# Forget gates placed between the second pair's keys and queries, with work tiles from another buffer pool

## The chip, the cores and the metric

The kernel runs on one core of a Trainium2 chip. The metric is device time in microseconds (us) per execution. A core has five instruction queues that work side by side and wait for each other through semaphores: TensorE (PE; its weight loads are shown apart as PEld), VectorE (DVE), ScalarE (ACT), GpSimd (POOL) and SyncE (SP), which here only issues DMAs. Each engine takes its own queue strictly in order.

## The reference

One layer of a streaming encoder for 512 new positions and, beside them, 64 positions that continue a stream with 1024 cached ones. Two kinds of attention share one input projection; FoX is the one that the change touches. Its logits carry a forget gate per head, a running sum F of log-sigmoids:

```python
h = rmsnorm(x, g_attn)
z = h @ w_in
q, k, v, f_lin, q_c, c_kv, k_r = jnp.split(z, IN_SPLIT_POINTS, axis=-1)
logf = jax.nn.log_sigmoid(f_lin.astype(jnp.float32) + b_f.astype(jnp.float32))
f_past = jnp.cumsum(plogf32, axis=1)
f_new = jnp.sum(plogf32, axis=1, keepdims=True) + jnp.cumsum(logf, axis=1)
...
s = jnp.einsum('bqhd,bkhd->bhqk', q, k, preferred_element_type=jnp.float32) * (FOX_DIM ** -0.5)
s = s + jnp.transpose(fq, (0, 2, 1))[:, :, :, None] - jnp.transpose(fk, (0, 2, 1))[:, :, None, :]
p = jax.nn.softmax(jnp.where(mask, s, NEG), axis=-1)
```

The second kind (MLA) follows with its own latents, then the output projection, a gated convolution block with an up and a down projection, and a final norm. `logf`, keys, values and latents are outputs too.

## The kernel before

All matrices lie transposed, features on partitions and the 576 positions along a row. Every product is made exact to about float32 by splitting both factors into a leading half and a remainder. For weights this is `hilo`: a weight tile of 128x1024 is loaded into `wr` (L185), ScalarE copies the leading half into `wh` (L194), and VectorE or GpSimd, in turn, writes the remainder (L135). `in_tile` then makes one 128-row tile of the projection: 48 matmuls (L210), 24 for each half of the positions, into two PSUM banks. There are two `wr` and two `wh` buffers, and two banks of the kind `g`.

`fox_gemm(p)` projects a pair of heads: keys, queries, values, each `in_tile` followed by two evictions on VectorE (L450, L454, L457) into a `raw` tile. There are seven `raw` buffers. Eight `mix` buffers hold the input `x` first (`x_in`), later the rotary key, the gate logits `z`, the latent tiles (`latent`, L541, five of them) and the attention outputs.

`gates` makes F out of `z` on 8 partitions: ScalarE adds the bias (L560), VectorE takes the minimum of z and -z (L562), ScalarE its exponential (L564), VectorE 1 + e and its rounding error (L566, L567), GpSimd a subtraction (L568), ScalarE the logarithm (L569), VectorE the sum (L570) and `logf` (L572), then the scans (L577 for the new positions, L586 for the 64 of the running stream), and ScalarE and VectorE split the sums into halves: L580 and L581 into `Fh`, `Fl` (tiles `qr`), L589 and L590 into `Fs` (tile `cf`). SyncE copies rows of `Fh` and `Fl` into each head's score tile `A` (L510, L511, `fox_stack`); the sample scores read `cf` directly (L523 of `fox_sample_scores`), after the product of cached keys and query (L522). Head scores are L515, L516 and a mask (L359), in four blocks of query rows per head, 256, 256, 384 and 512 wide; ScalarE takes the exponentials (L326), and TensorE transposes the result (L375).

What sets the order: generators (`s_gemm`, `s_scores`, `s_values`, `s_sample_scores`, `s_sample_values`) write the parts of the program by due times, and that writing order is a priority. When the kernel is built, a scheduler orders each engine's queue by priority and by what it reckons to be ready, and gives each tile a buffer of its kind that is free. So moving a call moves its instructions on every queue, and others around them. `s_gemm` is the generator that calls `fox_gemm(1)` first and then `gates`.

Of the kernel before, what the change touches and what calls it, by code (L numbers as in the profile page):

```python
# [17 lines left out]
T = NP + NS  # L18
# [53 lines left out]
def build(nc, tc, io):  # L72
# [7 lines left out]
    def f(ap):  # L80
        return ap.bitcast(F32)
# [6 lines left out]
    def raw():  # L88

        if ffn[0]:  # L90
            rawn[0] += 1
            tag, bufs = FRAW[rawn[0] % len(FRAW)]
            return sb([P, 580], F32, tag, bufs)
        return sb([P, 580], F32, "raw", RAW)

    def mixt():
        return sb([P, T], F32, "mix", 8)
# [194 lines left out]
    def in_tile(u, M=P):  # L292
        hl = wload(io["w_in"][u], 1024)
        ps = psg()
        gemm(ps, M, hl, xhl, HA)
        return ps
# [147 lines left out]

    mixes = [None] * 8

    def fox_gemm(p):
        ps = k0 if p == 0 else in_tile(p)
        k = raw()
        evac(lambda d, p, c: V.tensor_tensor(d, p, R[:, c], op=ALU.mult), k, ps)  # L450
        G.dma_start(io["o_k"][p], k[:, :T])
        ps = in_tile(4 + p)
        q = raw()
        evac(lambda d, p, c: V.scalar_tensor_tensor(d, p, FOX_SCALE, R[:, c], op0=ALU.mult, op1=ALU.mult), q, ps)  # L454
        ps = in_tile(8 + p)
        v = raw()
        evac(lambda d, p, c: V.tensor_tensor(d, p, R[:, c], op=ALU.mult), v, ps)  # L457
        G.dma_start(io["o_v"][p], v[:, :T])
        return q, k, v
# [96 lines left out]
    fx = {0: fox_gemm(0)}  # L556
    gate = {}

    def gates():
        S.activation(z, z, AF.Identity, bias=bf)  # L560
        mn = raw()[:8, :T]
        V.scalar_tensor_tensor(mn, z, -1.0, z, op0=ALU.mult, op1=ALU.min)  # L562
        e = raw()[:8, :T]
        S.activation(e, mn, AF.Exp)  # L564
        up = raw()[:8, :T]
        V.tensor_scalar(up, e, 1.0, None, op0=ALU.add)  # L566
        V.tensor_scalar(mn, up, 1.0, None, op0=ALU.subtract)  # L567
        G.tensor_tensor(e, e, mn, op=ALU.subtract)  # L568
        S.activation(up, up, AF.Ln)  # L569
        V.tensor_tensor(up, up, e, op=ALU.add)  # L570
        logf = raw()[:8, :T]
        V.scalar_tensor_tensor(logf, z, 0.0, up, op0=ALU.min, op1=ALU.subtract)  # L572
        G.dma_start(io["o_logf"], logf)
        zero8 = sb([8, 2816], F32, "B", 2)
        G.memset(zero8, 0.0)
        fp = raw()[:8, :T]
        V.tensor_tensor_scan(fp[:, :NP], logf[:, :NP], zero8[:, :NP], 0.0, op0=ALU.add, op1=ALU.add)  # L577
        Fhl = sb([8, 2, T], F32R, "qr", 1)
        Fh, Fl = Fhl[:, 0], Fhl[:, 1]
        S.activation(Fh[:, :NP], fp[:, :NP], AF.Copy)  # L580
        V.tensor_tensor(Fl[:, :NP], fp[:, :NP], f(Fh[:, :NP]), op=ALU.subtract)  # L581
        lc = sb([8, 1152], F32, "sp", 1)
        G.dma_start(lc[:, :PAST], io["logf_c"])
        fs = sb([8, 1152], F32, "spt", 1)
        V.tensor_tensor_scan(fs[:, :PAST], lc[:, :PAST], zero8[:, :PAST], 0.0, op0=ALU.add, op1=ALU.add)
        V.tensor_tensor_scan(fs[:, PAST:KEYS], logf[:, NP:T], zero8[:, :NS], fs[:, PAST - 1:PAST], op0=ALU.add, op1=ALU.add)  # L586
        Fs = sb([72, 1152], F32R, "cf", 1)
        G.memset(f(Fs), 0.0)
        S.activation(Fs[0:8, :KEYS], fs[:, :KEYS], AF.Copy)  # L589
        V.tensor_tensor(Fs[64:72, :KEYS], fs[:, :KEYS], f(Fs[0:8, :KEYS]), op=ALU.subtract)  # L590
        gate.update(h=Fh, l=Fl, s=Fs)
# [151 lines left out]
    def s_gemm():  # L743
        for p in range(1, 4):
            if p >= 2:
                yield ("after", ("stack", 2 * (p - 2) + 1), 0)
            fx[p] = fox_gemm(p)
            if p == 1:
                gates()
            yield ("done", 23.1, ("up", p))  # L750
            if p == 1:
                for a in range(5):
                    latent(a)
                    if a == 2:
                        rope_key()
                    if a == 1:
                        acc_c = sq_sum(craw)
                    if a == 4:
                        acc_q = sq_sum(qcr)
                    yield ("done", 7.7, ("lat", a))  # L760
            if p == 2:
                latent_norm(craw, 256, C_GKV, acc_c)
                latent_norm(qcr, 384, C_GQ, acc_q)
                for a in range(2):
                    G.dma_start(io["o_lat"][a], craw[a])
        mla_keys()
        yield ("done", 0, ("keys", 0))
        for p in range(4):
            if p == 0:
                yield ("after", ("stack", 5), 0)  # L770
            else:
                yield ("after", ("stack", 6 + 2 * p - 1), 0)
            if p % 2 == 0:
                q_rope(p // 2)
                yield ("done", 2.2, ("rope", p))
            mla_up(p)
            yield ("done", 5, ("up", 4 + p))
# [320 lines left out]
```

## Time and profile before

| | us |
|---|---|
| median of 3 runs (807.28 to 808.03) | 807.97 |
| the profiled execution | 810.69 |
| its span, first to last instruction | 808.9 |
| TensorE busy in it | 772.8 |
| VectorE busy | 508.5 |
| ScalarE busy | 340.6 |
| GpSimd busy | 264.0 |

The profiled execution is one run of its own, with a time of its own; the rows below are from it. A busy TensorE is not a TensorE at its peak: the granted clock says at which of its two levels it ran. The share of busy time over the whole span mixes stages with different limits, so the rows are given by stage and by engine.

### The profile page before, as it was taken

To read this page: it belongs to the slowest core of one execution; us is meant where nothing else is said; L and a number is where in the kernel's file an instruction comes from. 1 tells how busy PE (TensorE), PEld (TensorE's weight loads), DVE (VectorE), ACT (ScalarE), POOL (GpSimd) and SP (SyncE) were. 2 spreads that over 40 slices of the span, in tenths; PEclk is the share of its full clock that TensorE was granted. 3 is DMA by queue.
4 is the path that set the end of the run, shared out by engine and by line. 5 is a ranking of instruction groups with operands and counts; after the bars stand their busy time and mean duration, and the time that the engine had idled before them with its cause. 6 is when DMAs were issued, how large, how long until landed. Compare 5 with 4: busy or idle time off the path is not lost.

```text
span 808.9 us, 14256 instructions
## 1 busy us (share of the span) xinstructions
PE 772.8 (96%) x5582; PEld 743.3 (92%) x5582; DVE 508.5 (63%) x941; ACT 340.6 (42%) x611; POOL 264.0 (33%) x390
## 2 busy tenths in 40 slices
PE   8898999999899989999999999999999999999994
PEld 8796899897789879999999999999999999999993
DVE  6838554878677763457867524676425667675356
ACT  7224652457667864124443212343113433433231
POOL 5134342336143230223333221433222343332034
PEclk9998999999999999999999999999999999999997
DMA  9373423545563741222222223222232222222313
GB/s 329 111 212 109 109 84 106 145 107 169 129 152 80 185 131 30 80 79 79 72 85 68 79 92 105 79 79 60 79 98 80 103 80 79 79 66 83 105 40 117
DMA packets 33811, 83.98 MB, mean 104 GB/s; under 512 B 6006, under 2 KB 9350, under 8 KB 33744
## 3 DMA queue, kind: packets, MB, share of 16 engines
q1 hardware_dynamic: 31520, 78.55, 32.6%
q0 software_dynamic: 1008, 3.19, 1.1%
q10 hardware_dynamic: 1216, 1.33, 0.5%
q8 instruction: 44, 0.72, 0.4%
q14 instruction: 23, 0.19, 0.1%
HBM read 64.12 MB, written 5.49 MB: 86 GB/s over the span
## 4 chain that ended last, share of the span: by engine, by line
PE 76%; DVE 10%; ACT 5%; DMA 3%; issue 3%; SPq 1%; POOL 1%; DVEq 0%; ACTq 0%; POOLq 0%
PE g L210 31%; PE s L210 19%; PE t L210 12%; PE g L438 3%; PE g L969 1%; DMA mix<-xT 1%; DVE B L382 1%; DVE xs L267 1%; PE s L720 1%; PE t L375 1%; ACT p L326 1%; PE s L969 1%; DMA A<-qr 1%; PE s L522 1%; DVE raw L135 1%
## 5 line engine op out<-in xcount | busy, mean ns | idle before, releaser
L210 PE MATMUL g<-xs,wh 128*128 128x288 f32 (+2 forms) x2028 | 281.1, 295 | 0.3 <-ACT spt L128 0.2
L210 PEld LDWEIGHTS g<-xs,wh 128*128 128x128 f32 x2028 | 271.1, 189 | 1.7 <-ACT spt L128 0.4
L194 ACT ACTIVATE wh<-wr 128x1024 fp32r<-128x1024 f32 (+4 forms) x106 | 99.8, 942 | 204.3 <-PE g L210 88.4
L135 POOL TENSOR_TENSOR wh<-wr,wh 128x1024 fp32r<-128x1024 f32 (+3 forms) x51 | 111.8, 2192 | 216.5 <-ACT wh L194 173.7
L210 PE MATMUL s<-xs,wh 128*128 128x320 f32 (+3 forms) x840 | 121.1, 300 | 2.3 <-DVE xs L267 2.3
L210 PEld LDWEIGHTS s<-xs,wh 128*128 128x128 f32 (+1 forms) x840 | 116.3, 188 | 2.7 <-ACT wh L194 1.8
L210 PE MATMUL t<-xs,wh 128*128 128x256 f32 (+3 forms) x576 | 83.9, 296 | 1.2 <-DVE xs L267 1.2
L210 PEld LDWEIGHTS t<-xs,wh 128*128 128x128 f32 (+1 forms) x576 | 79.1, 188 | 1.6 <-DVE xs L267 1.4
L135 DVE TENSOR_TENSOR wh<-wr,wh 128x1024 fp32r<-128x1024 f32 (+5 forms) x55 | 59.0, 1077 | 13.7 <-ACT wh L194 13.4
L892 POOL COPY KR<-raw 128x2 f32<-128x2 f32 x33 | 14.6, 443 | 94.1 <-DVE raw L890 94.1
L332 POOL TENSOR_SCALAR p<-p,small 128x128 f32<-128x128 f32 (+2 forms) x48 | 27.5, 575 | 50.9 <-DVE small L327 40.8
L896 DVE SCALAR_TENSOR_TENSOR raw<-raw,par 128x578 f32<-128x578 f32 x22 | 33.6, 1526 | 14.0 <-ACT raw L895 14.0
L326 ACT ACTIVATE p<-s,small 128x128 f32<-128x128 f32 (+1 forms) x64 | 33.6, 527 | 12.5 <-DVE small L361 9.2
L920 ACT ACTIVATE raw<-raw 128x578 f32<-128x578 f32 x22 | 15.1, 688 | 54.5 <-DVE raw L897 54.5
L382 DVE TENSOR_TENSOR B<-t,B 128x512 fp32r<-128x512 f32 (+1 forms) x64 | 29.9, 482 | 9.3 <-ACT B L128 9.2
L128 ACT ACTIVATE B<-t 128x512 fp32r<-128x512 f32 (+1 forms) x64 | 26.2, 435 | 17.1 <-PE t L375 16.4
L361 DVE TENSOR_REDUCE small<-s 128x1 f32<-128x128 f32 (+1 forms) x64 | 30.5, 480 | 4.3 <-PE s L359 2.9
L896 DVE SCALAR_TENSOR_TENSOR raw<-pq,par,raw 128x578 f32<-128x578 f32 x11 | 22.7, 2059 | 12.4 <-ACT raw L895 12.4
L375 PE MATMUL t<-ident,p 128*128 128x128 f32 x160 | 29.1, 277 | 1.0 <-DVE B L382 0.5
L890 DVE TENSOR_TENSOR raw<-s,R 128x256 f32<-128x256 f32 x22 | 9.3, 424 | 31.8 <-PE s L210 31.8
L438 PE MATMUL g<-spt,sv 128*128 128x128 f32 x216 | 26.7, 276 | 0.3 <-ACT spt L128 0.2
L438 PEld LDWEIGHTS g<-spt,sv 128*128 128x128 f32 x216 | 25.2, 192 | 1.1 <-ACT spt L128 0.6
(337 smaller groups left out, 1344.1 us busy)
## 6 DMA issues: line engine op xcount, KB each, us to landing
wr<-w_up SPq DMA_DIRECT2D x44, 512.0 KB
wr<-w_dn SPq DMA_DIRECT2D x24, 384.0 KB
wr<-w_in SPq DMA_DIRECT2D x16, 512.0 KB
A<-pq SPq DMA_DIRECT2D x32, 256.0 KB
mix<-xT SPq DMA_DIRECT2D x16, 288.0 KB
wr<-w_out SPq DMA_DIRECT2D x8, 512.0 KB
A<-pq SPq DMA_DIRECT2D x24, 128.0 KB
sk<-k_c SPq DMA_DIRECT2D x4, 512.0 KB
```

Source lines behind the costliest of these rows:

```text
L128: S.activation(dst, src, AF.Copy)
L135: (V if pick(kind) == "v" else G).tensor_tensor(dst, a, b, op=op)
L194: S.activation(hl[:, 0, a:b], r[:, a:b], AF.Copy)
L210: PE.matmul(ps[hf][:M, :w], lhsT=hl[:, wi, kc * M:(kc + 1) * M], rhs=acts[kc][:, xi, o:o + w], start=(kc == 0 and pi == 0), stop=(kc == n ...
L326: S.activation(p, src, AF.Exp, bias=nm, accum_out=sm[:, 0:1])
L332: (G if e == "g" else V).tensor_scalar(p, p, sm[:, 1:2], 1.0, op0=ALU.mult, op1=ALU.mult)
L361: V.reduce_max(nm[:, 0:1], s[:, :W], axis=AX.X, negate=True)
L375: PE.transpose(t[:, P * (i - j):P * (i - j + 1)], st["p"][i][:, P * j:P * (j + 1)], ident)
L382: V.tensor_tensor(ptj[:, 1, off:], t[:, :w], f(ptj[:, 0, off:]), op=ALU.subtract)
L438: PE.matmul(out, lhsT=v[:, j, :], rhs=spt[:, j, :], start=(j == 0), stop=(j == 8))
L896: V.scalar_tensor_tensor(t, u[:, 1:579], par[:, C_CW + 44 + ch:C_CW + 44 + ch + 1], t, op0=ALU.mult, op1=ALU.add)
L969: PE.matmul(ps[:, :w], lhsT=whl[m][:, wi, kc * P:(kc + 1) * P], rhs=g2[kc][:, xi, c], start=(kc == 0 and pi == 0), stop=(kc == n - 1 and p ...
```

## The change

`fox_gemm` takes a second argument, a function that it calls between the keys and the queries. For pair 1 (the second) `s_gemm` passes `gates`, which it called after the whole of `fox_gemm(1)` before. And the five work tiles of `gates` come from `mixt()`, the `mix` buffers, and no longer from `raw()`.

```diff
-    def fox_gemm(p):
+    def fox_gemm(p, between=None):
         ps = k0 if p == 0 else in_tile(p)
         k = raw()
         evac(lambda d, p, c: V.tensor_tensor(d, p, R[:, c], op=ALU.mult), k, ps)
         G.dma_start(io["o_k"][p], k[:, :T])
+        if between:
+            between()
         ps = in_tile(4 + p)
...
-        mn = raw()[:8, :T]
+        mn = mixt()[:8]
...
-        e = raw()[:8, :T]
+        e = mixt()[:8]
...
-        up = raw()[:8, :T]
+        up = mixt()[:8]
...
-        logf = raw()[:8, :T]
+        logf = mixt()[:8]
...
-        fp = raw()[:8, :T]
+        fp = mixt()[:8]
...
-            fx[p] = fox_gemm(p)
-            if p == 1:
-                gates()
+            fx[p] = fox_gemm(p, gates if p == 1 else None)
```

The two lines added in `fox_gemm` push the later lines down by two: from L450 on, a line of the kernel before has a number higher by 2 in the kernel after (L523 becomes L525), up to the call in `s_gemm`. The rest of the text uses the numbers of before. What this does to the queues is shown at three places.

TensorE, from the first product of cached keys and query to the first head scores. L210 are projection matmuls, L341 and L494 transposes of values, L523 the sample scores that read the gates' sums. Before:

```order
L522 MATMUL s<-sk,qb 128x320
L210 MATMUL g<-xs,wh 128x288 x144
L341 MATMUL t<-ident,raw 128x128 x4
L494 MATMUL t<-ident,raw 64x128
L210 MATMUL g<-xs,wh 128x288 x27
L341 MATMUL t<-ident,raw 128x128 x4
L210 MATMUL g<-xs,wh 128x288 x10
L494 MATMUL t<-ident,raw 64x128
L210 MATMUL g<-xs,wh 128x288 x11
L523 MATMUL s<-cf,sl 128x384 x2
L523 MATMUL s<-cf,sl 128x320
```

And after:

```order
L524 MATMUL s<-sk,qb 128x320
L210 MATMUL g<-xs,wh 128x288 x72
L341 MATMUL t<-ident,raw 128x128 x2
L210 MATMUL g<-xs,wh 128x288 x24
L341 MATMUL t<-ident,raw 128x128 x2
L496 MATMUL t<-ident,raw 64x128
L525 MATMUL s<-cf,sl 128x384 x2
L525 MATMUL s<-cf,sl 128x320
L527 LDWEIGHTS bfc
L527 MATMUL s<-bfc 128x64
L210 MATMUL g<-xs,wh 128x288 x48
L517 MATMUL s<-A 128x256
```

The sample scores stand behind 96 projection matmuls instead of 192, and 48 of the others stand between them and the first head's scores; the last 48 of the 192 stand between that head's blocks, 30 of them ahead of the second head.

VectorE, where the gates' first instructions stand (L450, L454 and L457 are evictions of keys, queries and values, L465 and L467 splits for a pair's scores). Before, behind the weight remainder for the second pair's values:

```order
L467 TENSOR_TENSOR pq<-raw,pq 128x512
L454 SCALAR_TENSOR_TENSOR raw<-g,R 128x288 x2
L465 TENSOR_TENSOR pq<-raw,pq 128x512
L457 TENSOR_TENSOR raw<-g,R 128x288
L562 SCALAR_TENSOR_TENSOR raw<-mix 8x576
L566 TENSOR_SCALAR raw<-raw 8x576
L567 TENSOR_SCALAR raw<-raw 8x576
L457 TENSOR_TENSOR raw<-g,R 128x288
```

And after, behind the weight remainder for its keys:

```order
L564 SCALAR_TENSOR_TENSOR mix<-mix 8x576
L469 TENSOR_TENSOR pq<-raw,pq 128x512
L459 TENSOR_TENSOR raw<-g,R 128x288
L467 TENSOR_TENSOR pq<-raw,pq 128x512
L568 TENSOR_SCALAR mix<-mix 8x576
L459 TENSOR_TENSOR raw<-g,R 128x288
L569 TENSOR_SCALAR mix<-mix 8x576
L450 TENSOR_TENSOR raw<-g,R 128x288
L572 TENSOR_TENSOR mix<-mix 8x576
L574 SCALAR_TENSOR_TENSOR mix<-mix 8x576
L579 SCALAR_TENSOR_TENSOR mix<-mix,B 8x512
L588 SCALAR_TENSOR_TENSOR spt<-mix,spt,B 8x64
```

The gates' first three instructions stood behind the queries' evictions and the split of the second pair (L467, L465) and now stand among the first pair's; L570 to L586 stand between the two evictions of the second pair's keys (the first L450 is in the fence, the second follows it).

ScalarE, from the first pair's last split (L464) on; L194 are leading halves of weights. Before, up to the first exponential of a head:

```order
L464 ACTIVATE pq<-raw 128x512
L564 ACTIVATE raw<-raw 8x576
L194 ACTIVATE wh<-wr 128x1024
L569 ACTIVATE raw<-raw 8x576
L580 ACTIVATE qr<-raw 8x512
L589 ACTIVATE cf<-spt 8x1088
L194 ACTIVATE wh<-wr 128x1024
L220 ACTIVATE raw<-mix 128x576
L326 ACTIVATE p_683,small<-s,small 128x128
```

And after, the gates' part:

```order
L466 ACTIVATE pq<-raw 128x512
L566 ACTIVATE mix<-mix 8x576
L194 ACTIVATE wh<-wr 128x1024
L571 ACTIVATE mix<-mix 8x576
L194 ACTIVATE wh<-wr 128x1024
L582 ACTIVATE qr<-mix 8x512
L591 ACTIVATE cf<-spt 8x1088
L468 ACTIVATE pq<-raw 128x512
L194 ACTIVATE wh<-wr 128x1024
```

Four gate instructions moved from between the weight halves of the first three latent tiles to between those of the second pair's queries and values. The third latent tile's half, which followed the gates' last cast, now follows the first head's exponentials and those of the first sample.

## Rows read from the trace of the kernel before

**Rows 1.** Stages: us; busy us of each engine (instructions), clock, DMA share, GB/s.

```profile
42.10:113.80 71.70, 67.04 (x471) 61.58 (x470) 45.05 (x108) 35.50 (x79) 30.83 (x39) 0.95 0.45 123
113.80:145.60 31.80, 31.80 (x242) 31.80 (x241) 12.80 (x16) 6.80 (x11) 7.70 (x8) 1.00 0.38 115
318.60:808.90 490.30, 476.81 (x3565) 474.36 (x3563) 291.29 (x460) 162.84 (x208) 152.33 (x239) 0.99 0.26 82
```

**Rows 2.** Timeline, TensorE: start us, us, instructions [idle before <-releaser].

```profile
41.72 19.48 PE L210 MATMUL g<-xs,wh 128*128 128x288 f32 x144
...
66.94 1.71 PE L210 MATMUL g<-xs,wh 128*128 128x288 f32 x11
71.79 0.90 PE L523 MATMUL s<-cf,sl 72*128 72x384 f32 x3 [3.13 <-DVE cf L590]
...
72.89 0.58 PE L515 MATMUL s<-A 128*128 128x256 f32 x1
...
79.24 0.60 PE L375 MATMUL t<-ident,p 128*128 128x128 f32 x4
80.38 0.50 PE L515 MATMUL s<-A 128*128 128x512 f32 x1 [0.53 <-ACT p L326]
...
82.68 0.35 PE L516 MATMUL s<-A 66*128 66x256 f32 x1 [0.49 <-DMA A<-qr]
```

**Rows 3.** Timeline, TensorE's weight loads, at the first head's scores.

```profile
72.89 0.29 PEld L515 LDWEIGHTS s<-A 128*128 128x128 f32 x1 [0.26 <-DVE sp L410]
```

**Rows 4.** One microsecond: TensorE busy us, granted clock, DMA share, GB/s.

```profile
78.00:79.00 1.00, 1.00 (x6) 0.50 1.01 213
```

**Rows 5.** Timeline, TensorE at the upper clock level, the same forms.

```profile
87.23 0.49 PE L375 MATMUL t<-ident,p 128*128 128x128 f32 x3
...
88.31 0.36 PE L515 MATMUL s<-A 128*128 128x256 f32 x1
...
88.67 0.42 PE L515 MATMUL s<-A 128*128 128x384 f32 x1
...
89.16 0.90 PE L210 MATMUL g<-xs,wh 128*128 128x288 f32 x5
...
90.38 0.39 PE L515 MATMUL s<-A 128*128 128x512 f32 x1
...
90.88 1.83 PE L210 MATMUL g<-xs,wh 128*128 128x288 f32 x12
```

**Rows 6.** Timeline, the gates' instructions and what stands around them.

```profile
35.20 0.76 ACT L560 ACTIVATE mix<-mix,bf 8x576 f32<-8x576 f32 x1
...
40.38 1.06 ACT L194 ACTIVATE wh<-wr 128x1024 fp32r<-128x1024 f32 x1 [2.83 <-issue]
...
41.70 2.42 POOL L135 TENSOR_TENSOR wh<-wr,wh 128x1024 fp32r<-128x1024 f32 x1
...
45.32 0.46 DVE L450 TENSOR_TENSOR raw<-g,R 128x288 f32<-128x288 f32 x1 [4.53 <-PE g L210]
...
48.52 1.06 ACT L194 ACTIVATE wh<-wr 128x1024 fp32r<-128x1024 f32 x1 [7.08 <-PE g L210]
...
49.61 1.23 DVE L135 TENSOR_TENSOR wh<-wr,wh 128x1024 fp32r<-128x1024 f32 x1 [0.40 <-ACT wh L194]
...
61.89 1.42 POOL L568 TENSOR_TENSOR raw<-raw 8x576 f32<-8x576 f32 x1 [3.39 <-issue]
...
64.92 0.74 DVE L570 TENSOR_TENSOR raw<-raw 8x576 f32<-8x576 f32 x1
...
67.22 1.20 DVE L577 TENSOR_TENSOR_SCAN raw<-raw,B 8x512 f32<-8x512 f32 x1
...
70.45 1.28 DVE L590 TENSOR_TENSOR cf<-spt,cf 8x1088 fp32r<-8x1088 f32 x1
```

**Rows 7.** Timeline, VectorE: one form, alone and beside a GpSimd remainder.

```profile
50.91 0.69 DVE L467 TENSOR_TENSOR pq<-raw,pq 128x512 fp32r<-128x512 f32 x1
...
57.08 1.97 DVE L465 TENSOR_TENSOR pq<-raw,pq 128x512 fp32r<-128x512 f32 x1 [1.74 <-ACT pq L464]
```

## The prediction

> **What bounds the kernel now.** I read the stages first, then TensorE's instructions in the stage that the change touches, then the engines that feed it. The stage table [rows 1] says where time can be had at all. From 113.8 to 145.6 us TensorE is busy for the whole stretch, and from 318.6 us to the end for 476.8 of 490.3 us. In the stage that holds the forget gates, 42.1 to 113.8 us, it is busy for 67.04 of 71.70 us, so 4.66 us are idle, and the mean granted clock is 0.95 of full, so some of the busy time is slow as well. TensorE's own timeline [rows 2] shows why. It runs the second pair's keys, queries and values (144 matmuls from 41.72 us) and the first latent tile without a gap, and its last matmul there begins in the row of 66.94 us and is over 1.71 us later, at 68.65. Then it stands for 3.13 us, released by VectorE's L590, the last instruction of the gates: the next thing in its queue is the first sample-score matmul that reads the gates' sums. After that wait the granted clock is down: between 78 and 79 us it is still 0.50, the lower of the two levels (1.2 instead of 2.4 GHz) [rows 4]. So the first head scores and transposes run at half rate, and two smaller waits follow at 80.38 and 82.68 us [rows 2].
>
> So late gates cost twice: a wait, and slow work behind it. The gates are late because their first VectorE instruction stands behind the second pair's last split in the order, not because their input is late: ScalarE had biased the logits by 35.20 + 0.76 = 35.96 us [rows 6].
>
> **The change part by part.** *Buffers.* The five work tiles come out of the eight input-tile buffers. In the new order the first gate instruction stands before both evictions of the second pair's keys, and nothing but the biased logits is ahead of it that it needs. I cost the buffers at nothing: the input tiles are dead once their squares are summed, before TensorE's 144 matmuls start. If a latent tile had to wait for one of these buffers it would first show at its eviction some 20 us later.
>
> *Order.* No instruction is added, removed or made larger; about a dozen small ones move. On VectorE the product L570 now stands directly behind the first eviction of the second pair's keys, which ends at 45.32 + 0.46 = 45.78 [rows 6]. Its operand from GpSimd (L568, 1.42) queues behind the remainder of the query weights, 41.70 + 2.42 = 44.12, so it comes at 45.54 [rows 6]; ScalarE's logarithm stands between two weight halves and is done before that. From 45.78 VectorE needs 0.74 for L570, the same for L572 (same 8x576 form), 1.20 for the scan and 0.46 for the second eviction of the keys: 48.92. Two short ones (a 64-column scan and a copy) fit in the 0.69 left until 49.61, where the value weights' remainder ran before; its leading half came from ScalarE at 48.52 + 1.06 = 49.58 in either case [rows 6]. So nothing is pushed back there. Behind the remainder (50.84) come L581, bounded by the scan's 1.20 since it has the same 512 columns, and L590 with 1.28: the sums are ready by 53.3 [rows 6]. ScalarE's two casts have the sizes of these two subtractions and start earlier, at 49.58 against 50.84, so they do not decide.
>
> When does TensorE ask? The sample scores now stand behind 96 matmuls and five transposes instead of 192 and ten. 144 took 19.48 [rows 2], so 96 take 13.0, and from 41.72 that is 54.7 without the transposes. The sums are 1.4 us early at least. The 3.13 us wait goes. What would be late next is the first head's gate rows: SyncE's queue issues them after the first cast. The second latent tile's weight load now stands between them, so it waits for that cast, and its halves are not made before the value matmuls have released a buffer, some 48 matmuls after the scores. Both are hidden by those 48 matmuls, 6.5 us, which stand between the sample scores and the first head; with that cover gone the rows would cost about what their wait of 0.49 at 82.68 shows.
>
> *The sum.* (a) The wait, 3.13. (b) A weight load waits 0.26 at 72.89 for VectorE to empty a bank of the sample scores [rows 3]; behind the 48 matmuls it goes. (c) Half-rate work: from 72.89 to 79.24 are the scores of seven query blocks and three transposes, 6.35 us [rows 2]. At full rate a 256-wide block takes 88.67 - 88.31 = 0.36, a 384-wide one 89.16 - 88.67 = 0.49, the 512-wide one 90.88 - 90.38 = 0.50 [rows 5]; four, two and one are 2.92, and three transposes at most 0.49 [rows 5]: 3.41. The excess is 2.94. (d) The waits at 80.38 and 82.68, 0.53 and 0.49. Of these the first is a score bank waiting for ScalarE; in the new order ScalarE has a weight half (1.06 [rows 6]) ahead of the same exponentials, so it may come back whole; I count it, since 30 matmuls now stand before the head that needs it. The second ends with the third head's gate rows, which TensorE reaches later relative to the first head's end; it goes. Sum: 3.13 + 0.26 + 2.94 + 0.53 + 0.49 = 7.35.
>
> The bounds: 6.3 if (d) stays, and 4.66 + 2.94 + 0.26 = 7.86 if all idle time of the stage goes [rows 1]. From about 107 us on, all five queues have the same order in both kernels, and TensorE is the bound right behind that (113.8 to 145.6); a lead won before is carried to the end, since the loads too are released by the work before them. The profiled execution took 810.69 us (span 808.9), 2.72 above the median of the three runs, 807.97. So the profiled one would become 803.3, and the median 807.97 - 7.35 = **800.6 us**.
>
> *A rule against it.* In the row of 57.08 a two-operand split on VectorE (L465) takes 1.97 us; the same form at 50.91 takes 0.69 [rows 7]. During the slow one GpSimd was making a weight remainder. The Trainium skill (SBUF — State Buffer, "Who interferes with whom") says that a VectorE instruction with two SBUF inputs and a GpSimd instruction that reads SBUF exclude each other for the whole instruction; this trace agrees, with 1.97 against 0.69. By that rule the early gates would be at risk, since most of them have two such inputs; the sum by it would be unchanged as long as they fall after 45.54, where GpSimd is done reading, and otherwise it is the second rival.
>
> **The rivals.** *Part is given back.* The lead reaches a part of the stage (73 to 100 us) where ScalarE and GpSimd now also do the third latent tile's weight halves, which used to fall into the gap: 1.06 on ScalarE and at least 2.42 on GpSimd [rows 6] stand ahead of the second head's exponentials and of its scaling. For it speaks the wait of 0.53, which was of this kind; against it that several matmuls or transposes stand between. If both show on TensorE's path, 3.5 us come back: 804.1.
>
> *Gates still late.* The margin is 1.4 us, and one exclusion costs 1.97 - 0.69 = 1.28 [rows 7]. With two or three of them TensorE waits 1.2 to 2.4 us at the sample scores; if the clock falls behind it too, another 2.94. Take 3.6: 804.2. Against it: GpSimd reads nothing between 45.5 and the next remainder, which waits for the query matmuls at about 55.
>
> *Slower.* VectorE works in order, and L570 waits for GpSimd and ScalarE, both behind the query weights, which come by DMA: ScalarE took up the leading half at 40.38 only after waiting for them. Behind L570 on VectorE now stands the eviction of the keys' second bank, and the queries' second half cannot start without that bank, at 41.72 + 72/144 x 19.48 = 51.5. Gate work and eviction behind GpSimd's product take 0.74 + 0.74 + 1.20 + 0.46 = 3.14, so up to 48.3 nothing happens; that is 2.8 after 45.54. For the kernel to be slower the loss has to exceed 7.35, that is 4.4 of waiting and 2.94 of half rate, so the query weights would have to land over 7.2 us later than they did. At 10 us it would be 7.2 + 2.94 - 7.35 = 2.8 more than before, 810.8. Nothing in the order of the loads before that weight tile changes, so I give it little.
>
> *It does not do what it says.* Should a buffer be held after all (a late reader of an input tile), the gates stay where they were and the time with them: 808.
>
> **How the numbers follow.** Forecast 0.70 (own range 799.4 to 801.7: the bounds 6.3 and 7.86, and 0.69 for the fastest run, 807.28, below the median); part given back 0.16; gates still late 0.06; unchanged 0.04; slower 0.04. The range goes up to 804.0, which leaves out the worst of the second and third case and the last two: 799.4 to 804.0. A measurement here tells 0.2%, 1.6 us, from no change: below 806.4 is faster. Faster 0.92, same 0.04, slower 0.04.
>
> **What would show it.** Right: TensorE has no wait at the sample scores, these lie near 55 us, its clock stays at its upper level from 42 us through the head scores, the stage's idle time is under 1 us, and the stretch that TensorE fills from 113.8 us [rows 1] begins near 106.4. Wrong in (c): the clock falls although no wait of about 3 us is seen. Part given back: a wait by a score or transpose matmul on ScalarE or GpSimd between 73 and 100 us. Gates late: VectorE's last gate instruction ends after 55 us and releases TensorE. Slower: an L210 matmul of the queries waits for an eviction near 51 us. The forecast as a whole is wrong if that stretch starts 7 us sooner and the end does not come sooner; then a later stage is paced by something that does not move with them.

## The result and the profile after

The changed kernel takes 801.08 us (median of four runs, 800.27 to 803.26) against 807.62 for the kernel before beside it (four runs, 806.84 to 808.03): a ratio of 0.9922, 95% interval 0.9905 to 0.9938. The forecast was 800.6 in a range of 799.4 to 804.0. The time came out close to it; the account of where it comes from did not hold in all parts, as the experiments show, so the closeness of the number is in part luck.

The profiled execution of after took 800.29 us, with a span of 798.4. The first view is the table of stages of after (columns as in [rows 1]). The first row answers to the first of [rows 1], the second to the stretch from 113.8 us; the windows are those of this execution's own clock, so they do not hold quite the same work as before.

```profile
42.10:106.00 63.90, 63.81 (x476) 60.00 (x476) 42.89 (x106) 34.37 (x79) 27.78 (x39) 1.00 0.49 140
106.00:137.80 31.80, 31.80 (x231) 30.76 (x230) 16.46 (x26) 8.36 (x12) 7.96 (x7) 1.00 0.42 119
```

TensorE is idle for 0.09 us of the stage where it was idle for 4.66, and its granted clock is at its upper level throughout (1.00 instead of 0.95).

The second view is TensorE's timeline in after, the rows that answer to [rows 2].

```profile
36.54 1.99 PE L524 MATMUL s<-sk,qb 128*128 128x384 f32 x6
51.55 0.74 PE L525 MATMUL s<-cf,sl 72*128 72x384 f32 x3
52.18 6.61 PE L210 MATMUL g<-xs,wh 128*128 128x288 f32 x48
58.62 0.28 PE L517 MATMUL s<-A 128*128 128x256 f32 x1
...
67.29 0.71 PE L375 MATMUL t<-ident,p 128*128 128x128 f32 x5
...
98.14 1.45 PE L390 MATMUL g<-B,v 128*128 128x512 f32 x8
...
101.36 1.83 PE L210 MATMUL g<-xs,wh 128*128 128x288 f32 x12
```

No row has a wait in brackets. The sample scores (L525, L523 before) come at 51.55 us, 48 projection matmuls stand behind them, and the run of projections that began at 113.56 in before begins at 101.36.

VectorE's rows in after say when the gates were done, against [rows 6]:

```profile
42.10 0.73 DVE L572 TENSOR_TENSOR mix<-mix 8x576 f32<-8x576 f32 x1
...
47.91 1.28 DVE L592 TENSOR_TENSOR cf<-spt,cf 8x1088 fp32r<-8x1088 f32 x1
```

The last gate instruction ends at 49.19, 2.36 us before TensorE asks.

**Two executions that start differently.** In after everything lies some 3.6 us earlier before the change can act: the first cached-key product is at 36.54 (above), while it was at 40.13 in the profiled execution before. So a row of after must be compared from that product on. I use as "the stage" the stretch from it (L522, in after L524) to the first product L390 into a bank `g`, in the second head pair. Its rows, before first, then after (same columns):

```profile
40.13:110.34 70.21, 65.55 (x450) 59.49 (x449) 43.60 (x106) 34.91 (x78) 29.19 (x39) 0.95 0.48 134
```

```profile
36.54:98.14 61.60, 61.51 (x450) 57.10 (x449) 42.01 (x105) 33.91 (x77) 29.18 (x39) 1.00 0.54 153
```

The same 450 matmul records take 8.61 us less: 4.57 of idle time and 4.04 of busy time. That is 1.3 more than the 7.35 of the prediction. Part of it is lost later. The next rows are the stretch from the first score with the rotary key (tile `KR`) to the first matmul L210 that reads tile `A` into a bank `s`, in the convolution block: before, and then after, with a stretch inside it.

```profile
212.76:452.36 239.60, 230.93 (x1661) 220.58 (x1660) 158.84 (x310) 119.45 (x238) 73.82 (x113) 1.00 0.32 93
```

```profile
200.58:441.77 241.19, 232.52 (x1662) 221.87 (x1661) 158.95 (x310) 119.43 (x238) 73.76 (x113) 0.99 0.32 93
209.52:212.94 3.42, 3.42 (x12) 2.92 (x11) 3.42 (x11) 3.01 (x11) 0.94 (x1) 0.50 0.40 123
```

After has a stretch of half clock at 209.5 us that before has not, and takes 1.59 us longer for the same work. 8.61 - 1.59 leaves 7.0, beside 7.35 forecast and 6.54 between the medians.

### The profile page after: what moved, and what is told of

Same layout as the page of the kernel before. It is cut to its first block, busy times and chain, and to the rows that moved or that the text cites. A ratio compares the mean times of both kernels' runs of the same rounds, so it can differ in the third digit from the quotient of the medians.

```text
span 798.4 us, 14254 instructions
## 1 busy us (share of the span) xinstructions
PE 770.1 (96%) x5582; PEld 743.0 (93%) x5582; DVE 505.9 (63%) x941; ACT 340.4 (43%) x611; POOL 263.9 (33%) x390
## 4 chain that ended last, share of the span: by engine, by line
PE 83%; DVE 6%; ACT 4%; DMA 3%; issue 2%; SPq 1%; POOL 0%; DVEq 0%; ACTq 0%
PE g L210 36%; PE s L210 20%; PE t L210 13%; PE g L438 3%; PE g L969 1%; PE s L722 1%; PE t L375 1%; DVE xs L267 1%; ACT p L326 1%; PE s L969 1%; DVE B L382 1%; PE o L390 1%; DMA A<-pq 1%; PE s L524 1%; PE t L969 1%
## 5 line engine op out<-in xcount | busy, mean ns | idle before, releaser
L210 PE MATMUL g<-xs,wh 128*128 128x288 f32 (+2 forms) x2028 | 282.0, 295 | 0.2
L210 PEld LDWEIGHTS g<-xs,wh 128*128 128x128 f32 x2028 | 271.6, 189 | 1.3 <-DVE xs L135 0.4
L194 ACT ACTIVATE wh<-wr 128x1024 fp32r<-128x1024 f32 (+4 forms) x106 | 99.8, 943 | 208.4 <-PE g L210 87.3
L210 PE MATMUL s<-xs,wh 128*128 128x320 f32 (+3 forms) x840 | 121.5, 301 | 1.9 <-DVE xs L267 1.9
L210 PEld LDWEIGHTS s<-xs,wh 128*128 128x128 f32 (+1 forms) x840 | 116.5, 188 | 2.4 <-ACT wh L194 1.4
L210 PE MATMUL t<-xs,wh 128*128 128x256 f32 (+3 forms) x576 | 84.2, 297 | 1.2 <-DVE xs L267 1.2
L210 PEld LDWEIGHTS t<-xs,wh 128*128 128x128 f32 (+1 forms) x576 | 79.3, 188 | 1.6 <-DVE xs L267 1.4
L326 ACT ACTIVATE p<-s,small 128x128 f32<-128x128 f32 (+1 forms) x64 | 33.6, 527 | 7.7 <-DVE small L361 6.0
```

The costliest lines, as they stand in the source:

```text
L194: S.activation(hl[:, 0, a:b], r[:, a:b], AF.Copy)
L210: PE.matmul(ps[hf][:M, :w], lhsT=hl[:, wi, kc * M:(kc + 1) * M], rhs=acts[kc][:, xi, o:o + w], start=(kc == 0 and pi == 0), stop=(kc == n ...
L326: S.activation(p, src, AF.Exp, bias=nm, accum_out=sm[:, 0:1])
```

## The experiments

All times stand beside runs of the kernel before on the same chip: medians 808.73 (e1 to e4), 808.58 (e5 to e8) and 808.26 (e9 to e12). The table's last three columns are from the profiled execution of each: where the first cached-key product starts, the length of the stage, and the stretches of half clock between 40 and 780 us.

| kernel | median us (runs) | ratio to before, 95% | first product at | stage | half clock |
|---|---|---|---|---|---|
| before | 807.62 (4) | | 40.13 | 70.21 | 72.3 to 79.1 |
| after | 801.08 (4) | 0.9922 (0.9905 to 0.9938) | 36.54 | 61.60 | 209.5 to 212.9 |
| e1_buffers | 800.38 (6) | 0.9897 (0.9877 to 0.9918) | 36.35 | 61.60 | 208.6 to 212.0 |
| e2_order | 803.85 (12) | 0.9944 (0.9925 to 0.9963) | 38.05 | 64.25 | none |
| e3_filler3 | 813.64 (6) | 1.0063 (1.0041 to 1.0084) | 37.83 | 74.39 | 69.0 to 79.2, 103.1 to 106.5, 222.6 to 226.0 |
| e4_start | 799.57 (6) | 0.9888 (0.9866 to 0.9910) | 36.33 | 61.60 | 208.5 to 211.9 |
| e5_fill128 | 810.81 (10) | 1.0022 (1.0005 to 1.0040) | 39.92 | 73.38 | 76.7 to 86.9 |
| e6_crowd2 | 801.17 (4) | 0.9903 (0.9876 to 0.9931) | 37.03 | 61.59 | 210.4 to 213.8 |
| e7_crowd6 | 800.21 (4) | 0.9896 (0.9866 to 0.9926) | 36.23 | 62.63 | none |
| e8_split | 800.61 (6) | 0.9894 (0.9870 to 0.9917) | 36.45 | 61.60 | none |
| e9_fill_late | 807.32 (10) | 0.9996 (0.9979 to 1.0013) | 36.86 | 70.15 | none |
| e10_crowdlong | 803.84 (9) | 0.9941 (0.9920 to 0.9961) | 36.23 | 66.17 | 54.4 to 57.8 |
| e11_after | 801.17 (6) | 0.9913 (0.9885 to 0.9941) | 36.77 | 61.60 | 209.7 to 213.1 |
| e12_start | 799.51 (6) | 0.9892 (0.9870 to 0.9915) | 36.30 | 61.59 | none |

The stage is a sharp measure: 61.59 to 61.60 us in all seven profiles whose kernels leave it as the change made it, whatever their start.

### Which half of the change does it: e1 and e2

e1 is the changed kernel with the call put back:

```diff
-            fx[p] = fox_gemm(p, gates if p == 1 else None)
+            fx[p] = fox_gemm(p)
+            if p == 1:
+                gates()
```

> Only the five work tiles are taken from the input tiles' buffers; the gates are called where the kernel before calls them, after all three tiles of the second pair. Theory A (the prediction's wording: the gates were late because they stood behind the second pair's last split in the order written): nothing moves, 807.6 us, and the 3.1 us wait at the first sample score stays. Theory B (the gates were late because their tiles had to wait for one of the seven working buffers): the place of the call means nothing, all queues come out in the same order as in the changed kernel, and the time is the changed kernel's, 801.1 us give or take 1.5.

Theory B. With the buffers alone the order of the instructions on all five engines is that of the changed kernel, the stage is 61.60 and the time is 800.38. Where the call stands changes nothing, once the tiles are free to be had. What had kept the gates behind the queries' evictions (VectorE's order before the change, above) was that their tiles had to come from the seven `raw` buffers.

e2 keeps the new place and gives the five tiles back to `raw()` (`mn`, `e`, `up`, `logf`, `fp`).

> Only the place of the call is changed; the five work tiles still come from the seven working buffers. The gates' VectorE instructions stand some 6 to 8 places earlier than before, and the sample scores behind 144 of the matmuls instead of 96 (192 before). Theory A (the place does it): 801 us. Theory B (the buffers do it): the gates are still behind the releases of the working buffers; if the sums nevertheless come before TensorE has done the 144 matmuls (asked at about 61.5 us of the profile before), the wait goes too and the time is 801 to 802; if they come 1 to 3 us later than that, a wait of that size stays, with a slow stretch behind it, 804 to 808.

Here neither theory has it whole. The place alone also brings the gates forward, since they then ask for `raw` buffers ahead of the queries and values; but less. The rows are TensorE's in e2:

```profile
59.50 0.66 PE L525 MATMUL s<-cf,sl 72*128 72x384 f32 x3
...
72.61 0.50 PE L517 MATMUL s<-A 128*128 128x512 f32 x1 [1.49 <-ACT p L326]
```

The wait at the sample scores is gone, but they stand behind 48 projection matmuls more. 48 of these instead of 96 are left between the sample scores and the second head, and TensorE waits 1.49 us for ScalarE's exponentials, ahead of which ScalarE now does a weight half and a sample's exponential. The stage is 64.25: 5.96 us gained instead of 8.61.

### What the late sums cost: e3, e5 and e9

The prediction had a wait of 3.13 us and 2.94 us of half-rate work behind it, as two losses to be added. These three kernels are the kernel before with extra matmuls in that wait, so that the gates come no sooner but TensorE has work.

e3 takes three matmuls on the gates' own 8-row tile:

```diff
+        fill = bank("o")
+        for n in range(3):
+            PE.matmul(fill[:, :T - 64], lhsT=up[:, :P], rhs=up[:, :T - 64], start=True, stop=True)
```

> The kernel before with three extra matmuls of 8 x 512 in float32 (estimated 0.85 us each, from 0.39 us for each of the two passes of a 384-wide one in the trace of before) on the gates' intermediate tile, into a bank that nobody uses then. They stand seven matmuls before TensorE's 3.1 us wait, so TensorE works for about 2.6 us of it and nothing else moves. Theory A (a large part of the loss is the slow clock behind the wait, 2.9 to 3.5 us): the clock stays at its upper level through the head scores and the time falls from 807.6 to 804.2 (ratio 0.9957), although the sums come no sooner. Theory B (only the waits count, the slow stretch is hidden behind other engines): 807.6, or up to 808 with the fillers' own time.

TensorE's timeline in e3, and a window of it:

```profile
65.34 2.84 PE L580 MATMUL o<-raw 8*128 8x512 f32 x6
...
69.40 1.27 PE L523 MATMUL s<-cf,sl 72*128 72x384 f32 x3
...
73.62 0.69 PE L515 MATMUL s<-A 128*128 128x384 f32 x1 [1.28 <-DVE sp L410]
```

```profile
69.00:79.24 10.24, 8.96 (x35) 6.36 (x33) 7.89 (x23) 5.84 (x15) 4.90 (x7) 0.50 0.38 99
```

The wait at the sample scores was filled, and the clock fell to its lower level all the same, at 69.0 us, behind 2.84 us of matmuls that use 8 of the 128 rows, and for 10.24 us instead of 6.83. TensorE then waited 1.28 us for a bank: VectorE's cast L499, ahead of the copy that empties it, took 2.07 us beside a GpSimd remainder that ran until 73.11. The time was 813.64, slower than before (ratio 1.0063), where 804.2 or 807.6 to 808 was expected. With the clock down, e3 did not separate the theories. e5 took matmuls of the projections' form instead.

```diff
+        fill = bank("o")
+        PE.matmul(fill[:, :8], lhsT=up[:, :P], rhs=up[:, :8], start=True, stop=True)
+        for n in range(20):
+            PE.matmul(fill[:, :288], lhsT=xhl[0][:, 0, :P], rhs=xhl[1][:, 0, :288], start=True, stop=True)
```

> The kernel before with 20 extra matmuls of the projections' own form (128 rows, 288 columns, 0.135 us each in its trace, 2.7 us) seven matmuls before TensorE's 3.1 us wait; a matmul of 8 columns ahead of them ties them to the gates' time. The extra matmuls with only 8 rows (e3) filled the same gap, and the clock fell all the same, for 10.2 us. Theory A (the clock falls because TensorE has little to do there, and rows count too): with full matmuls the clock stays at its upper level from 69 to 80 us, the stretch from the first cached-key product to the first product of the second head pair's values falls from 70.2 to 66.2 to 66.8 us, and the time lies 3.4 us under the kernel before (ratio 0.9958). Theory B (the clock falls for the wait alone, or at that place in any case): it falls as before, and the stretch stays at 70 us or more.

Rows of e5: TensorE, then VectorE and GpSimd, and the same two instructions before.

```profile
71.42 0.66 PE L523 MATMUL s<-cf,sl 72*128 72x384 f32 x3
...
75.79 0.44 PE L515 MATMUL s<-A 128*128 128x384 f32 x1 [2.13 <-DVE sp L410]
```

```profile
72.95 2.38 DVE L499 CAST sl<-sel 72x64 fp32r<-72x64 f32 x1
```

```profile
72.87 2.41 POOL L135 TENSOR_TENSOR wh<-wr,wh 128x1024 fp32r<-128x1024 f32 x1 [1.34 <-ACT wh L194]
```

```profile
73.23 0.83 DVE L499 CAST sl<-sel 72x64 fp32r<-72x64 f32 x1
```

```profile
71.12 2.89 POOL L135 TENSOR_TENSOR wh<-wr,wh 128x1024 fp32r<-128x1024 f32 x1 [3.60 <-ACT wh L194]
```

The clock stayed up through the sample scores, but the last projection matmuls stood behind the extra ones, so a weight remainder of GpSimd began 1.75 us later than before and lay on the whole of VectorE's cast L499 (before, only its end at 74.01 did). The cast ended with it, the bank behind it was emptied late, TensorE waited 2.13 us, and the clock fell there. The filler had made another wait, and the time was 810.81, slightly slower than before (1.0022). e9 puts the same 20 matmuls directly ahead of the sample scores and ties them to a later scan (`fs` in place of `up`).

> As e5, but the 20 matmuls (2.7 us) stand directly before the first sample score, behind all of the projections' matmuls, and are tied to the last scan of the gates. In e5 they stood seven matmuls earlier; so the weight buffer came free later, GpSimd's weight remainder moved from 71.1 to 72.9 us, onto VectorE's copy L499, which then took 2.38 us instead of 0.83, TensorE waited 2.13 us for the bank behind it, and the clock fell there. Now nothing else should move. Theory A (the slow clock behind the wait is a loss of its own): TensorE waits at most 0.5 us at the sample score, the clock stays up, and the stretch from the first cached-key product to the first product of the second head pair's values falls from 70.2 to 66.2 to 67 us. Theory B (VectorE, ScalarE and GpSimd pace this stretch whatever TensorE's clock is): the clock stays up, new waits on these engines take its place, and the stretch stays at 69 to 71.

This is the clean one. TensorE in e9, then the stage and the stretch from the sample scores to the first product of values, then that stretch before:

```profile
65.77 2.90 PE L590 MATMUL o<-xs 128*128 128x288 f32 x20
68.51 0.76 PE L523 MATMUL s<-cf,sl 72*128 72x384 f32 x3
69.61 0.39 PE L515 MATMUL s<-A 128*128 128x256 f32 x1 [0.29 <-DVE sp L410]
...
71.23 0.44 PE L515 MATMUL s<-A 128*128 128x384 f32 x1 [0.57 <-DVE sp L410]
...
76.47 0.50 PE L515 MATMUL s<-A 128*128 128x512 f32 x1 [0.61 <-ACT p L326]
...
79.35 0.36 PE L516 MATMUL s<-A 66*128 66x256 f32 x1 [0.54 <-DMA A<-qr]
```

```profile
36.86:107.01 70.15, 67.14 (x472) 60.60 (x471) 43.30 (x106) 34.89 (x78) 29.12 (x39) 1.00 0.49 134
68.51:80.42 11.91, 9.31 (x51) 5.92 (x50) 7.97 (x27) 6.94 (x21) 7.23 (x11) 1.00 0.60 139
```

```profile
71.79:83.74 11.95, 10.76 (x49) 7.76 (x50) 8.18 (x27) 6.94 (x21) 7.25 (x11) 0.71 0.57 134
```

With the clock at 1.00 instead of 0.71 the stretch takes 11.91 us instead of 11.95, and the stage 70.15 instead of 70.21. The time is that of the kernel before (0.9996). Theory B: with the half rate gone, next to nothing was won. A faster TensorE only waits more (2.60 us idle in the stretch instead of 1.19): for VectorE's copies out of the score banks (L410), for an exponential of ScalarE (L326) and for the rows of the third head's tile `A`. In the chain of work that ended last, both stretches end with SyncE's issues of these rows and their DMA, e9 first, then before:

```profile
73.99 1.69 SPq L477
...
77.08 2.18 DMA A<-qr
```

```profile
77.83 0.63 SPq L477
...
80.52 2.06 DMA A<-qr
```

Counted from the sample scores, SyncE began these issues at 4.29 us in e9 (72.80) and at 4.85 before (76.64), 0.56 sooner, and then lost that lead, one issue (L477) taking 1.69 us instead of 0.63. So up to some 0.6 us of cost of the half rate is not ruled out by this one profile; 2.94 is.

### How late the gates may be: e6, e7 and e10

These are the changed kernel with GpSimd made busy beside the gates, the queues of TensorE, VectorE and ScalarE staying in order. The core of e6 (two adds) and e7 (six), with `zero8` allocated earlier for it:

```diff
+        for n in range(2):
+            G.tensor_tensor(zero8[:, 1152:1728], e, e, op=ALU.add)
```

> The changed kernel with two more GpSimd adds of 8 x 576 (1.42 us each, reading SBUF, results unused) directly behind GpSimd's part of the gates, while VectorE does its own. The order on TensorE, VectorE and ScalarE is the same. In the profile after, the sums were ready at 49.2 and TensorE asked for them at 51.55: a margin of 2.3 us. Theory A (the two engines exclude each other there): VectorE's last gate instruction ends up to 2.8 us later, at 52.0, TensorE waits at most 0.5 us, and the time is the changed kernel's to within 0.6 us. Theory B (no exclusion): nothing moves, sums at 49.2. Either way the time is 800 to 801.5; the rows tell them apart.

> The same with six such GpSimd adds, 8.5 us. Theory A (exclusion): the sums come up to 8.5 us later, at 54 to 57.7 us, TensorE waits 3 to 6 us at the first sample score and the clock falls behind the wait: 3 to 6 us and another 3 to 4, so 806 to 811, as slow as the kernel before. Theory B (no exclusion): 800 to 801.5 and no wait.

VectorE's rows of the gates in e7, with the first sample score on TensorE behind them:

```profile
42.91 1.59 DVE L578 SCALAR_TENSOR_TENSOR mix<-mix 8x576 f32<-8x576 f32 x1
44.52 2.05 DVE L581 TENSOR_TENSOR_SCAN mix<-mix,B 8x512 f32<-8x512 f32 x1
46.51 1.16 DVE L590 TENSOR_TENSOR_SCAN spt<-mix,spt,B 8x64 f32<-8x64 f32 x1
...
49.29 1.63 DVE L585 TENSOR_TENSOR qr<-mix,qr 8x512 fp32r<-8x512 f32 x1
50.95 1.28 DVE L594 TENSOR_TENSOR cf<-spt,cf 8x1088 fp32r<-8x1088 f32 x1
```

```profile
52.29 0.76 PE L525 MATMUL s<-cf,sl 72*128 72x384 f32 x3 [0.42 <-DVE cf L594]
```

Four instructions (L578, L581, L590, L585) are 0.84 to 0.96 us longer than in after (there 0.74, 1.21, 0.31 and 0.67). Counted from the first cached-key product, the sums come 3.35 us later than in after in e7 and 1.30 in e6. So the exclusion is there, but smaller than forecast: four of the six adds ran beside the gates and lengthened one instruction each, by less than their own 1.4 us, and the last two ran from 52.57 us on, after the sums. The margin of 2.36 held for e6 (no wait, stage 61.59), and was just used up in e7: a wait of 0.42, a stage longer by 1.03, and a clock that stayed at its upper level. The 3 to 6 us of wait that theory A gave for e7 did not come.

e10 has two long adds in place of these:

```diff
+            G.tensor_tensor(zero8[:, 1152:], zero8[:, 1152:], e[:, 0:1].to_broadcast([8, 1664]), op=ALU.add)
```

> The changed kernel with two long GpSimd adds (8 x 1664, 4.1 us each by the 1.42 us of 576 columns) behind GpSimd's part of the gates, in place of the six short ones of e7, which made the sums 3.35 us late and left a wait of 0.42 us. Theory A (the loss before the change was the lateness of the sums): each long add holds one VectorE instruction of the gates for up to 4.1 us, the sums come between 53.3 and 57.4 us, TensorE waits 1.8 to 5.9 us at the first sample score, the clock falls behind it, and the stretch from the first cached-key product grows from 61.6 to 65 to 71 us. Theory B (the new order, with matmuls between sample scores and head scores, takes the wait without a slow stretch): only the wait itself is lost, 63.4 to 67.5, and the clock stays up.

Rows of e10: VectorE, TensorE, and the windows.

```profile
42.92 3.40 DVE L578 SCALAR_TENSOR_TENSOR mix<-mix 8x576 f32<-8x576 f32 x1
...
49.44 3.44 DVE L585 TENSOR_TENSOR qr<-mix,qr 8x512 fp32r<-8x512 f32 x1
```

```profile
54.25 1.19 PE L525 MATMUL s<-cf,sl 72*128 72x384 f32 x3 [2.24 <-DVE cf L594]
...
55.34 7.71 PE L210 MATMUL g<-xs,wh 128*128 128x288 f32 x48
```

```profile
36.23:102.40 66.17, 63.58 (x451) 58.55 (x449) 48.56 (x106) 34.24 (x77) 35.87 (x41) 0.97 0.51 144
54.40:57.80 3.40, 3.40 (x14) 3.15 (x15) 3.40 (x4) 0.00 (x0) 2.46 (x2) 0.50 0.03 5
```

The sums are 5.3 us later than in after, TensorE waits 2.24 us, and the clock falls behind the wait. Now the slow clock does cost: from the first sample score to the first head score it is 8.63 us (54.25 to 62.88) instead of 7.07 in after, 1.56 more, with 3.40 us of back-to-back matmuls at half rate in it that nothing but TensorE paces. The stage is 4.57 longer, 2.5 of it idle and 2.07 busy. Late sums, with the order of TensorE's queue as in after, bring back over half of what the change gained; theory A holds. The other 4.0 us stay gained in this order.

### What the start and the middle add: e4, e12, e11 and e8

e4 and e12 are the same kernel: after, with one weight remainder made by VectorE instead of GpSimd.

```diff
-        tt("wF" if ffn[0] else "w0" if wn[0] < W0 else "wA", hl[:, 1, a:b], r[:, a:b], f(hl[:, 0, a:b]), ALU.subtract)
+        if wn[0] == W0:
+            pick("wA")
+        tt("wF" if ffn[0] else "w0" if wn[0] <= W0 else "wA", hl[:, 1, a:b], r[:, a:b], f(hl[:, 0, a:b]), ALU.subtract)
```

> The changed kernel with one instruction moved: the remainder of the sixth weight slice, which GpSimd makes while VectorE adds the squares of the input (18 to 24 us), is made by VectorE. In the profile before, these two ran at the same time, VectorE's three sums took 5.67 us and TensorE waited 2.89 us for them; in the profile after, GpSimd's came later, the sums took 3.51 us, TensorE did not wait, and the first cached-key product came 3.59 us sooner (36.54 against 40.13). Theory A (whether the two overlap is luck of the run, and it is the spread of 3 us among the changed kernel's runs): the median falls to 800.3 and the spread to under 1 us. Theory B (the spread is set by something else, such as where the early stretch of slow clock falls): the median stays at 801 and the spread at 3 us. If VectorE's longer queue delays the norm, up to 1.2 us are lost: 802.

> The changed kernel itself, beside e12 on the same chip, for the start: expected 800.3 to 801.2. In its profile the first cached-key product is expected between 36.2 and 40.2 us; in those so far it came at 36.2 to 37.0 where VectorE's sums of squares and GpSimd's weight remainder did not overlap, 37.8 to 38.1 where the remainder overlapped VectorE's next instruction, and 40.1 and 39.9 (both with the old tiles) where it overlapped the sums.

> The kernel of e4 again, beside the changed kernel on the same chip. Theory A (the moved remainder takes the luck out of the start): 0.5 to 1.5 us under e11, largest time under 801. Theory B (the 0.8 us between e4 and e1 was chance): the same as e11 to within 0.4 us.

VectorE and GpSimd at the start of the kernel before, and then the same two in after:

```profile
18.71 5.67 DVE L135 TENSOR_TENSOR raw<-raw 128x576 f32<-128x576 f32 x3
```

```profile
21.43 2.34 POOL L135 TENSOR_TENSOR wh<-wr,wh 128x1024 fp32r<-128x1024 f32 x1 [0.68 <-ACT wh L194]
```

```profile
18.53 3.51 DVE L135 TENSOR_TENSOR raw<-raw 128x576 f32<-128x576 f32 x3
```

```profile
22.97 2.48 POOL L135 TENSOR_TENSOR wh<-wr,wh 128x1024 fp32r<-128x1024 f32 x1 [2.41 <-ACT wh L194]
```

Where GpSimd's remainder falls into VectorE's sums, these take 5.67 instead of 3.51 us, and the first cached-key product comes at 40.1 instead of 36.5. ScalarE's weight half ahead of the remainder goes with it: where it began at 18.91 (e5) and 19.11 us (before), the first product came at 39.92 and 40.13; at 19.30 (e3) and 19.53 (e2), at 37.83 and 38.05; from 19.99 to 21.15 (the other seven profiles with the remainder on GpSimd), at 36.23 to 37.03. With the remainder on VectorE it began at 19.39 in e12, and the first product still came at 36.30. The 12 runs of e4 and e12 have a median of 799.54 (797.76 to 801.37), the 16 of the changed kernel (with e1, which has the same order) 800.76 (798.19 to 805.52); the means differ by 1.3 us, with 1.0 as twice its standard error. So this is a small gain of its own, and the fastest version here. That the spread is under 1 us was not borne out: some of it has other reasons. Four of the five profiles with `raw` tiles had the late start and none of the six with `mix` tiles and the remainder on GpSimd; whether the tiles have a part in that or it is chance was not tested. The stage, counted from the first cached-key product, is free of it; the times are not.

e8 adds to e4 that the second kind's sample keys are cast in two pieces:

```diff
+        for c in (slice(0, 384), slice(384, KEYS)):
+            S.activation(KS[0:32, c], krc[:, c], AF.Copy)
+            V.tensor_tensor(KS[32:64, c], krc[:, c], f(KS[0:32, c]), op=ALU.subtract)
+            S.activation(KS[64:96, c], krc[:, c], AF.Copy)
```

> The kernel of e4 with one more edit, far from the change: the second kind's sample keys are cast in two pieces (384 and 704 columns) instead of one of 1088, so that the first piece is ready sooner. In all profiles TensorE waits 1.77 to 2.5 us for them (at 208.34 in the profile after), and in the changed order a slow stretch of 3.4 us lies right behind (209.5 to 212.9), where 1.6 us of the lead are lost again. Theory A (the slow stretch comes of that wait): with the wait at 0.3 to 0.5 us the clock stays up, and 1.4 + 1.6 = 3.0 us are saved: 796.6. Theory B (the slow stretch has another reason): 1.4 us are saved and it stays: 798.2. Theory C (the queue behind is not faster for it): 799.6.

TensorE in e8 (the sample scores that read the keys are L726 here and L723 in after, the products of values L392 and L390):

```profile
206.99 0.41 PE L726 MATMUL s<-cf,sl 96*128 96x384 f32 x1 [0.53 <-ACT cf L643]
...
209.04 0.44 PE L392 MATMUL o<-B,v 128*128 128x384 f32 x1 [1.65 <-ACT B L128]
```

The wait for the keys fell to 0.53 us, and the next one, for ScalarE's copies behind the two extra pieces, took its place: theory C, with 800.61 for the 799.6 expected. The slow stretch was absent in this profile, but also in e7, e10 and e12, where the wait stood as it was. Of the nine profiles in the new order (e8's own differs a little there) five had it. The long stretch of which after's row is given above (241.19) takes 239.3 to 240.3 us without it and 240.9 to 241.6 with it, so it costs some 1.5 us where it comes. What decides whether it comes was not settled.

## Why the prediction was right, and where it was not

**The wait and the other idle time.** The 3.13 at the sample scores, the 0.26 and the two of 0.5 went, as said: 4.57 us of idle time against 4.41 summed. (The 0.26 is a weight load's; TensorE's matmuls stood for 0.12 of it, from 72.77 to 72.89, and the bound of 7.86 counts that part twice.) The gates' timing held as well. On the time scale of before (3.59 later) the sums came at 52.8 where 53.3 was the bound, and the sample scores at 55.1 where 54.7 plus some transposes was said.

**Why the gates were late.** Here the step was wrong: it was put down to the place of the call. e1 shows that the buffers alone bring the whole 8.61, e2 that the place alone brings 5.96. The prediction costed the buffers at nothing; with them the place adds nothing, and without them 2.65 us are missing.

**The term (c), half-rate work, 2.94.** The step that failed. The rows of 72.89 to 79.24 were at half clock, but e9 kept the clock up and the stage stayed at 70.15. The work there was paced by VectorE, which emptied score banks, by ScalarE, which made exponentials, and by SyncE's row loads. What the change brought is cover: 96 projection matmuls now lie between the sample scores and the second head, so that TensorE has work while those engines do this. No run changes the cover by itself; e2, with 48 such matmuls and a gain of 5.96, fits. The gain is therefore the whole difference between the stage and TensorE's own work in it, 70.21 - 61.60 = 8.61, and not a wait plus a slow clock. The sum of 7.35 was 1.26 short, and its upper bound of 7.86 too low: of the 4.04 us by which TensorE's busy time fell, e9 has still some 2.6 at full clock (67.14 - 3.06 - 61.51; the filler with the matmuls that tie it is busy for 3.06, from 65.45 to 68.51). One reading of this, which was not tested apart, is that matmuls standing alone count their whole length as busy: the same block starts with 0.39 in e9 and 0.28 in after.

**"Carried to the end".** Not wholly. Queues in equal order did keep the lead to about 209 us, and then 1.6 us of it was lost to a stretch of half clock that comes in about half of the profiles. This and the 1.26 nearly cancel, which is why 7.35 met the medians: the nearness is luck, made of a term that was wrong, a sum that was too small and a loss that was not foreseen.

**The profiled execution as a base.** 810.69 us held a late start of 3.6 us, so the 803.3 forecast for it has no counterpart, and the stretch forecast to begin near 106.4 began at 101.36; the step from the median, 807.97 - 7.35, was the right one.

**The rivals.** Part given back between 73 and 100 us: not in after; in e2 it is what happened, with a wait of 1.49 behind a weight half on ScalarE. Gates still late: the margin was 2.4 and not 1.4; with sums 5.3 us later, e10 took 803.84, beside the 804.2 worked out. Slower by the query weights: no sign of it in any profile; in e10 alone an L210 matmul waits 0.26 us at 48.22 for an eviction of the keys.

**The rule on VectorE and GpSimd.** With GpSimd's adds beside the gates, VectorE's two-input instructions took 0.8 to 2.8 us longer (e7, e10), and in e6 it was the margin that kept this off the time. In after itself they kept their lengths of before to 0.01 us (0.73 for L572, 0.74 for L570 before). The Trainium skill (SBUF — State Buffer, "Who interferes with whom") also lists casts among what can contend with GpSimd. The trace of e5 agrees: L499, a cast, took 2.38 us beside a remainder of 2.41; before, with only the end of a remainder on it, 0.83, and its second call 0.18 with none beside it.

## What to carry to other kernels

Where a scheduler assigns buffers, look first at which pool a late instruction's output comes from: here another pool brought the whole gain of 8.61, and the place of the call brought 5.96 alone and nothing once the pool was changed. To size what an earlier result is worth, compare the length of the stage with the bound engine's own work in it (not with its busy time, which was 4 us above that before the change), and ask what work will stand between the result and its reader: the sum of listed waits and of slow work counts some things that cost nothing and misses others. In these runs a slow clock cost time only where TensorE itself set the pace: some 0.6 us at most in 6.8 in the old order (e9), 1.6 us in 3.4 where matmuls stood back to back (e10).

## What the runs showed of the hardware beside this

The granted clock fell behind 2.84 us of matmuls that use 8 rows (e3) with no wait before it, some 0.9 us into the projection matmuls that followed them, and stayed up behind 2.90 us of matmuls with 128 rows in the same gap (e9); TensorE's row is full in both. The two fillers differ in width too (512 and 288 columns), so which difference matters is not shown. An exclusion between VectorE and GpSimd appears in the trace not as a wait but as a longer instruction: 3.40 us for one of 0.74 (e10). And a small lead can be a disadvantage: at the start of before, ScalarE's weight half came 1.5 us sooner than in after, GpSimd's remainder fell on VectorE's sums, and the first cached-key product came 3.6 us later.
